# The low part of a split weight chunk, made by an adding DMA instead of by GpSimd

## The chip, the cores and the metric

The kernel runs on one core of a Trainium2 chip. The metric is device time in microseconds (us) from one launch to its end; lower is better. The kernel before takes 1719.38 us (median of three runs, 1719.3 to 1720.42).

## The reference, cut to what matters

One layer of a decoder block on 512 tokens of width 1024: a token-mixing half (gated mixer, sliding-window attention, output projection, layer norm), then a PEER layer that picks 16 of 128 x 128 = 16384 one-neuron experts for each of 8 heads. The change lies in the PEER layer:

```python
q = (xb @ w_pq).reshape(-1, PEER_HEADS, PEER_QDIM)
s1 = jnp.einsum('thd,hkd->thk', q1, sub_k1)          # and s2
v1, i1 = lax.top_k(s1, PEER_TOPK)                    # and v2, i2
cand = v1[..., :, None] + v2[..., None, :]
sc, ci = lax.top_k(cand, PEER_TOPK)
g = jax.nn.softmax(sc, axis=-1)
act = jax.nn.gelu(jnp.einsum('thkd,td->thk', peer_u[e], xb))
return jnp.einsum('thk,thkd->td', g * act, peer_v[e])
```

## The kernel before, in words

Three of the four blocks of 128 tokens (384 tokens) are computed densely: all 16384 experts are applied to them, and the gates g of the experts that were not picked are zero. The table `peer_u` is cut into 128 chunks of 128 experts ("U chunks"), and `peer_v` likewise ("V chunks"). The fourth block of tokens gathers its rows of both tables by indirect DMAs from GpSimd (`ru`, `rv`) late in the program.

Every product is made of three matmuls in a format that keeps fewer bits than f32. A weight chunk is loaded as f32 (`raw`, 128 x 1024, 512 KB), ScalarE (ACT) copies it to the short format (`hi`), and the low part `lo = raw - hi` is made by an elementwise subtraction. `load_split2` does this; the flag `last["pool"]` says whether GpSimd (POOL, line 456) or VectorE (DVE, line 458) subtracts. The tiles rotate over 4 buffers of `raw`, 3 of `hi` and 3 of `lo`. TensorE (PE) then runs 8 times `hi*h2Thi` (L62), `hi*h2Tlo` (L63), `lo*h2Thi` (L64), and ACT applies gelu; while the top-k runs, `U_chunk` also stores the activations to memory (`Ad`, 192 KB, a DMA that ACT issues). SP issues the loads of `raw`, each as soon as the buffer of four chunks earlier has been read for the last time.

The order on each engine is fixed when the program is built. The part in question runs in these steps:

- 16 query projections (`query`, `scores`), with GpSimd subtracting.
- The top-k of all heads, some 250 small steps on DVE (`topk`, lines 533 to 582). Beside it PE computes U chunks: chunks 0 and 1 were made earlier, chunk 2 is issued with the last of the queries, and chunks 3 to 32 follow. GpSimd subtracts for all 31.
- `softmax` (lines 589 to 595: a subtraction on DVE, an exp on ACT, three DVE steps), and `end_topk`, after which DVE subtracts again.
- `spread` (lines 615 to 656): PE transposes the picked indices and gates (`ptg`), ACT copies them (`iT`, `gT`), DVE builds one-hot tiles (`oh`), PE multiplies them (`psg`), ACT copies the result out (`stg`). U chunks 33 and on run beside it, 21 of them with their activations kept in SBUF (`U_resident`).
- The remaining U chunks with the V chunks, and beside them the gathers.

Of the kernel before, what the change touches and what calls it, by code (L numbers as in the profile page):

```python
# [8 lines left out]
F32 = mybir.dt.float32  # L9
# [4 lines left out]
AF = mybir.ActivationFunctionType  # L14
ALU = mybir.AluOpType
# [39 lines left out]
def block_kernel(ctx, tc, I, out):  # L55
    nc = tc.nc
    PS = bass.MemoryType.PSUM

    def mm3(ps, pairs):
        n = len(pairs)  # L60
        for i, (l, r) in enumerate(pairs):
            nc.tensor.matmul(ps, l.hi, r.hi, start=(i == 0), stop=False)  # L62
            nc.tensor.matmul(ps, l.hi, r.lo, start=False, stop=False)  # L63
            last = nc.tensor.matmul(ps, l.lo, r.hi, start=False, stop=(i == n - 1))  # L64
        return last
# [43 lines left out]
    with ExitStack() as fr:  # L109
# [288 lines left out]
        for hh in range(2):  # L398
            for t in range(NT):
# [13 lines left out]
                for kh in range(2):  # L413
# [5 lines left out]
                    for k4 in range(4):  # L419
                        k = 4 * kh + k4  # L420
                        if k < NEV:
                            nc.scalar.activation(hf[:, k4, :], pt[:, k4 * P:(k4 + 1) * P], AF.Identity,
                                                 scale=G2c[:, k:k + 1], bias=B2c[:, k:k + 1])
# [11 lines left out]
    last = {}  # L435

    def behind(ins, other):

        tc.add_manual_dep(ins.ins, other.ins.name,
                          mybir.DependencyInfo(mybir.DependencyClass.NoSync, mybir.DependencyReason.DATA))  # L440
# [4 lines left out]
    def load_split2(src, nm, pool=None):  # L445
        raw = pw.tile([P, NK * P], F32, name=f"raw{nm}", tag="raw", bufs=4)
        last["dma"] = nc.sync.dma_start(raw, src)
        hi = (pool or pw).tile([P, NK * P], F32R, name=f"hi{nm}", tag="hi", bufs=1 if pool else 3)
        lo = (pool or pw).tile([P, NK * P], F32R, name=f"lo{nm}", tag="lo", bufs=1 if pool else 3)
        h = nc.scalar.activation(hi, raw, AF.Copy)  # L450
        if "expn" in last:
            last["expn"] -= 1
            if last["expn"] == 0:
                behind(last["exp"], h)
        if last.get("pool"):
            last["pool_lo"] = nc.gpsimd.tensor_sub(lo, raw, hi.bitcast(F32))  # L456
        else:
            last["dve"] = nc.vector.tensor_sub(lo, raw, hi.bitcast(F32))  # L458
        return Split(hi, lo)
# [11 lines left out]
    def pump(us):  # L471
        credit[0] += us
        while credit[0] > 0 and bg:
            try:
                credit[0] -= next(bg[0])
            except StopIteration:
                bg.pop(0)
# [38 lines left out]
    def query(h, half):  # L516
        nm = f"{h}_{half}"
        w = load_split2(I["w_pq"][2 * h + half], f"pq{nm}")
        ps = pu.tile([P, S], F32, name=f"psq{nm}", tag="mm", bufs=2)
        wv = Split(w.hi.rearrange("p (k c) -> p k c", k=NK), w.lo.rearrange("p (k c) -> p k c", k=NK))  # L520
        mm3(ps, [(wv[:, k, :], h2T[:, k, :]) for k in range(NK)])
        qt = tp.tile([P, S], F32, name=f"qt{nm}", tag="qt", bufs=2)
        nc.scalar.copy(qt, ps)
        return qt

    def scores(h, half, qt):
        pss = pq.tile([P, NT, P], F32, name=f"pssc{h}_{half}", tag="s", bufs=2)
        for t in range(NT):
            nc.tensor.matmul(pss[:, t, :], qt[:, t * P:(t + 1) * P], subk[:, half, h, :], start=True, stop=True)
        nc.scalar.copy(sall[:, 2 * h + half, :, :], pss)  # L530
# [67 lines left out]
    def topk_head(h):  # L598
        return topk(f"h{h}_", DENSE, lambda half, j: sall[:, 2 * h + half, j, :],
                    lambda a: a[:, 0:DENSE, 16 * h:16 * h + 16])  # L600
# [92 lines left out]
    def U_resident(i):  # L693

        w = load_split2(I["uT"][i], f"U{i}")
        ps = pu.tile([P, SD], F32, name=f"psU{i}", tag="mm", bufs=2)
        wv = Split(w.hi.rearrange("p (k c) -> p k c", k=NK), w.lo.rearrange("p (k c) -> p k c", k=NK))
        last["U"] = mm3(ps, [(wv[:, k, :], h2T[:, k, 0:SD]) for k in range(NK)])
        slot, n = res["tile"][:, len(res["ids"]), :], res["spread"]
        if n < SD:  # L700
            nc.scalar.activation(slot[:, n:], ps[:, n:], AF.Gelu)
        if n:
            a = actp.tile([P, SD], F32, name=f"act{i}", tag="act", bufs=4)
            nc.scalar.activation(a[:, 0:n], ps[:, 0:n], AF.Gelu)
            nc.vector.tensor_mul(slot[:, 0:n], slot[:, 0:n], a[:, 0:n])
        res["ids"].append(i)

    def U_chunk(i, keep_act):
        w = load_split2(I["uT"][i], f"U{i}")
        ps = pu.tile([P, SD], F32, name=f"psU{i}", tag="mm", bufs=2)  # L710
        wv = Split(w.hi.rearrange("p (k c) -> p k c", k=NK), w.lo.rearrange("p (k c) -> p k c", k=NK))
        last["U"] = mm3(ps, [(wv[:, k, :], h2T[:, k, 0:SD]) for k in range(NK)])
        a = actp.tile([P, SD], F32, name=f"act{i}", tag="act", bufs=4)
        nc.scalar.activation(a, ps, AF.Gelu)
        if not keep_act:
            nc.scalar.dma_start(Ad[i], a)
        return a
# [86 lines left out]
    bg.append(rows_h2())  # L804
    qt = query(0, 0)
    for j in range(16):
        nxt = query((j + 1) // 2, (j + 1) % 2) if j < 15 else U_chunk(NPRE, False)
        scores(j // 2, j % 2, qt)
        qt = nxt
        if j % 2 == 1:  # L810
            bg.append(topk_head(j // 2))
        pump(QPUMP)
# [5 lines left out]
    def end_topk():  # L818
        tk.close()
        last["pool"] = PLO > 1  # L820
        res["stack"] = ExitStack()
        rp = res["stack"].enter_context(tc.tile_pool(name="rp", bufs=1, side="right", reuse_waits="tile"))
        res["tile"] = rp.tile([P, NRES, SD], F32, name="res")
        res["ids"] = []
        res["first"] = cur[0] + 1
        res["spread"] = 0
        return
        yield

    def end_spread():  # L830
# [3 lines left out]
        yield  # L834

    bg += [topk_last(), softmax(), end_topk(), spread(), end_spread()]
    gt = gather()
    n_g = 0
# [140 lines left out]
```

## Time and profile before

| what | value |
|---|---|
| median of three runs | 1719.38 us |
| the profiled execution | 1727.59 us, span 1725.9 us |
| PE busy | 1668.0 us, 97% of the span |
| DVE busy | 1353.8 us, 78% |
| ACT busy | 685.9 us, 40% |
| POOL busy | 481.5 us, 28% |
| granted TensorE clock | 0.991 of full speed, mean |

The profile is of one execution, which took 8.2 us longer than the median of the runs without a profile; its durations are compared with each other, and a difference is then carried over to the median. Shares over the whole span are averages of stages with different limits. Matmuls are pipelined, so a matmul's duration is not the time that it costs: that is the distance from one start to the next. Times in the rows are microseconds from the start of the span.

### The profile page before, as it was taken

How to read it: one execution, taken by the hardware profiler on the slowest of the kernel's cores; microseconds unless marked ns; L12 is line 12 of the kernel's file. 1: busy time of each engine (PE TensorE's matmuls, PEld its weight loads, DVE VectorE, ACT ScalarE, POOL GpSimd, SP SyncE). 2: the span in 40 equal slices, each digit the busy share in tenths (PEclk: the TensorE clock that was granted, in tenths of full speed). 3: DMA queues.
4: the chain of work that ended last, by engine and by line, in shares of the span. 5: the costliest groups of instructions: out<-in, count | busy, mean ns of one | idle time of the engine just before them, and what ended most of it. 6: DMA issues, size and time to landing. Idle time of an engine off the chain costs nothing.

```text
span 1725.9 us, 23559 instructions
## 1 busy us (share of the span) xinstructions
PE 1668.0 (97%) x8658; PEld 1442.8 (84%) x8658; DVE 1353.8 (78%) x2509; ACT 685.9 (40%) x1095; POOL 481.5 (28%) x334
## 2 busy tenths in 40 slices
PE   6999999999999999899999999999999999989997
PEld 3765777788788999899998789999999999978886
DVE  6467786454589999999978888778787888878787
ACT  3467632233343333355543233333333333333333
POOL 2000000000043455400014444444454545531202
PEclk9999999999999999999999999999999999999999
DMA  7602257642252355556699999999899999899982
GB/s 269 201 1 74 98 196 245 219 146 86 77 189 78 103 173 172 191 206 224 211 321 365 363 325 340 320 338 351 312 337 324 326 345 324 311 351 316 305 282 86
DMA packets 162071, 409.92 MB, mean 238 GB/s; under 512 B 22337, under 2 KB 69473, under 8 KB 161698
## 3 DMA queue, kind: packets, MB, share of 16 engines
q1 hardware_dynamic: 112178, 245.35, 42.3%
q0 software_dynamic: 36960, 134.50, 21.6%
q10 hardware_dynamic: 12816, 28.55, 4.3%
q8 instruction: 68, 1.11, 0.3%
q14 instruction: 49, 0.40, 0.1%
HBM read 377.07 MB, written 31.01 MB: 236 GB/s over the span
## 4 chain that ended last, share of the span: by engine, by line
PE 55%; DVE 18%; DMA 5%; issue 4%; POOL 2%; ACT 0%; SPq 0%; DVEq 0%; POOLq 0%; ACTq 0%
PE acc L801 8%; PE acc L800 8%; PE acc L797 8%; PE psU L64 7%; PE psU L62 6%; PE psU L63 6%; DMA wa<-in_w_ada_dram 2%; POOL ru L667 2%; DMA ru<-in_peer_u_dram,idx 1%; DMA rawV<-in_peer_v_dram 1%; PE pso L63 1%; PE pso L64 1%; PE psga L64 1%; PE psga L62 1%; PE pspa L64 1%
## 5 line engine op out<-in xcount | busy, mean ns | idle before, releaser
L64 PE MATMUL psU<-h2Thi,loU 128*128 128x384 f32 x1008 | 340.6, 338 | 5.4 <-DVE loU L458 5.3
L62 PE MATMUL psU<-h2Thi,hiU 128*128 128x384 f32 x1008 | 340.8, 338 | 0.0
L63 PE MATMUL psU<-h2Tlo,hiU 128*128 128x384 f32 x1008 | 339.3, 337 | 0.0
L797 PE MATMUL acc<-hiV,wh 128*128 128x512 f32 x768 | 300.1, 391 | 4.5 <-ACT wh L782 4.5
L800 PE MATMUL acc<-loV,wh 128*128 128x512 f32 x768 | 301.5, 393 | 1.5 <-DVE loV L458 1.5
L801 PE MATMUL acc<-hiV,wl 128*128 128x512 f32 x768 | 301.1, 392 | 0.3 <-DVE wl L783 0.3
L667 POOL DMA_INDIRECT ru<-in_peer_u_dram,idx x128 | 159.0, 1242 | 360.6 <-DVE ru L671 341.2
L680 POOL DMA_INDIRECT rv<-in_peer_v_dram,idx x128 | 176.4, 1378 | 247.9 <-DVE facc L686 226.6
L458 DVE TENSOR_TENSOR loV<-rawV,hiV 128x1024 fp32r<-128x1024 f32 x128 | 156.4, 1222 | 101.2 <-ACT hiV L450 100.9
L450 ACT ACTIVATE hiV<-rawV 128x1024 fp32r<-128x1024 f32 x128 | 135.1, 1055 | 224.2 <-PE psU L63 184.1
L450 ACT ACTIVATE hiU<-rawU 128x1024 fp32r<-128x1024 f32 x126 | 134.0, 1063 | 194.5 <-PE psU L63 105.5
L64 PEld LDWEIGHTS psU<-h2Thi,loU 128*128 128x128 f32 x1008 | 190.4, 189 | 7.7 <-DVE loU L458 7.6
L63 PEld LDWEIGHTS psU<-h2Tlo,hiU 128*128 128x128 f32 x1008 | 190.6, 189 | 2.6
L62 PEld LDWEIGHTS psU<-h2Thi,hiU 128*128 128x128 f32 x1008 | 190.4, 189 | 2.6
L797 PEld LDWEIGHTS acc<-hiV,wh 128*128 128x128 f32 x768 | 144.9, 189 | 33.7 <-ACT wh L782 5.1
L671 DVE SCALAR_TENSOR_TENSOR ru<-ru,h2n 128x1024 f32<-128x1024 f32 x128 | 154.4, 1221 | 22.0 <-DMA ru<-in_peer_u_dram,idx 21.8
L800 PEld LDWEIGHTS acc<-loV,wh 128*128 128x128 f32 x768 | 144.8, 189 | 32.0 <-DVE loV L458 3.1
L801 PEld LDWEIGHTS acc<-hiV,wl 128*128 128x128 f32 x768 | 144.8, 189 | 31.1 <-DVE wl L783 0.7
L686 DVE SCALAR_TENSOR_TENSOR facc<-rv,wg,facc 128x1024 f32<-128x1024 f32 x126 | 159.4, 1278 | 11.7 <-DMA rv<-in_peer_v_dram,idx 11.7
L456 POOL TENSOR_TENSOR lopq<-rawpq,hipq 128x1024 fp32r<-128x1024 f32 x16 | 40.7, 2544 | 325.1 <-ACT hipq L450 325.1
L782 ACT ACTIVATE wh<-wf 128x384 fp32r<-128x384 f32 x107 | 56.2, 526 | 183.4 <-DVE wf L778 100.5
L458 DVE TENSOR_TENSOR loU<-rawU,hiU 128x1024 fp32r<-128x1024 f32 x95 | 115.7, 1218 | 1.4 <-ACT hiU L450 1.4
(628 smaller groups left out, 2942.4 us busy)
## 6 DMA issues: line engine op xcount, KB each, us to landing
rawU<-in_uT_dram SPq DMA_DIRECT2D x128, 512.0 KB
rawV<-in_peer_v_dram SPq DMA_DIRECT2D x128, 512.0 KB
wa<-in_w_ada_dram SPq DMA_DIRECT2D x48, 512.0 KB
G<-Gd SPq DMA_DIRECT2D x11, 1536.0 KB
Gd<-stg ACTq DMA_DIRECT2D x24, 592.0 KB
rawpq<-in_w_pq_dram SPq DMA_DIRECT2D x16, 512.0 KB
Ad<-act ACTq DMA_DIRECT2D x38, 192.0 KB
ar<-Ad SPq DMA_DIRECT2D x9, 768.0 KB
```

The costliest lines, as they stand in the source:

```text
L62: nc.tensor.matmul(ps, l.hi, r.hi, start=(i == 0), stop=False)
L63: nc.tensor.matmul(ps, l.hi, r.lo, start=False, stop=False)
L64: last = nc.tensor.matmul(ps, l.lo, r.hi, start=False, stop=(i == n - 1))
L450: h = nc.scalar.activation(hi, raw, AF.Copy)
L458: last["dve"] = nc.vector.tensor_sub(lo, raw, hi.bitcast(F32))
L667: d = nc.gpsimd.indirect_dma_start(out=rows, out_offset=None, in_=I["peer_u"], in_offset=bass.IndirectOffsetOnAxis(ap=idx[:, s:s + 1], axi ...
L671: paced(nc.vector.scalar_tensor_tensor(rows, rows, 1.0, h2n, op0=ALU.mult, op1=ALU.mult, accum_out=wg[:, s:s + 1]))
L680: nc.gpsimd.indirect_dma_start(out=rows, out_offset=None, in_=I["peer_v"], in_offset=bass.IndirectOffsetOnAxis(ap=idx[:, s:s + 1], axis=0))
L686: paced(nc.vector.scalar_tensor_tensor(fa, rows, wg[:, s:s + 1], fa, op0=ALU.mult, op1=ALU.add))
L797: m = nc.tensor.matmul(acc, l.hi, r.hi, start=st, stop=False)
L800: nc.tensor.matmul(acc, l.hi, r.lo, start=False, stop=False)
L801: nc.tensor.matmul(acc, l.lo, r.hi, start=False, stop=sp_)
```

## The change

While the top-k runs (from chunk 2 to chunk 32), `load_split2` makes `lo` in another way. ACT writes `-hi` into `lo` (a scaled copy, from `hi`), and a DMA issued by GpSimd adds `raw` to it, from SBUF to SBUF. GpSimd's subtraction is not made for these 31 chunks. The 16 query chunks keep it. All other instructions stay.

```diff
+        if last.get("dma_lo"):
+            nc.scalar.activation(lo, hi.bitcast(F32), AF.Copy, scale=-1.0)
+            last["pool_lo"] = nc.gpsimd.dma_start(lo.bitcast(F32), raw, accum_op=ALU.add)
-        if last.get("pool"):
+        elif last.get("pool"):
             last["pool_lo"] = nc.gpsimd.tensor_sub(lo, raw, hi.bitcast(F32))
...
     for j in range(16):
+        last["dma_lo"] = j == 15
...
     def end_topk():
+        last["dma_lo"] = False
```

The orders of PE, DVE and SP are the same in both kernels. On ACT, in the middle of the top-k, one chunk before is a copy to `hi` of a chunk, the gelu of the chunk three earlier (`act`), and the issue of the store of that one (`Ad`):

```order
L450 ACTIVATE hiU13_5131<-rawU13_5129 128x1024
L714 ACTIVATE act10_5012<-psU10_4987 128x384
L716 DMA Ad_77<-act10_5012 128x384
L450 ACTIVATE hiU14_5178<-rawU14_5176 128x1024
L714 ACTIVATE act11_5064<-psU11_5039 128x384
```

Now the negative copy stands between the gelu and the store:

```order
L450 ACTIVATE hiU13_5142<-rawU13_5140 128x1024
L717 ACTIVATE act10_5021<-psU10_4996 128x384
L456 ACTIVATE loU13_5143<-hiU13_5142 128x1024
L719 DMA Ad_77<-act10_5021 128x384
L450 ACTIVATE hiU14_5190<-rawU14_5188 128x1024
L717 ACTIVATE act11_5074<-psU11_5049 128x384
```

So ACT has one instruction more in each of the 31 chunks, and the low part of chunk 13 is begun behind the gelu of chunk 10. On POOL, the same chunks before:

```order
L456 TENSOR_TENSOR loU13_5132<-rawU13_5129,hiU13_5131 128x1024
L456 TENSOR_TENSOR loU14_5179<-rawU14_5176,hiU14_5178 128x1024
L456 TENSOR_TENSOR loU15_5227<-rawU15_5224,hiU15_5226 128x1024
```

and now:

```order
L457 DMA loU13_5143<-rawU13_5140 128x1024
L457 DMA loU14_5191<-rawU14_5188 128x1024
L457 DMA loU15_5240<-rawU15_5237 128x1024
```

Each subtraction has become the issue of one DMA in the same place.

## Rows read from the trace of the kernel before

**Rows 1.** Busy time by engine, granted clock, DMA share and rate in stretches.

```profile
588.20:718.20 130.00, 130.00 (x755) 130.00 (x755) 129.62 (x541) 46.83 (x66) 71.65 (x29) 1.00 0.48 163
718.20:728.60 10.40, 6.03 (x23) 5.38 (x22) 10.19 (x16) 3.48 (x5) 5.87 (x4) 0.67 0.60 206
...
760.00:790.00 30.00, 28.62 (x247) 27.26 (x246) 30.00 (x40) 16.14 (x33) 0.00 (x0) 1.00 0.63 222
```

**Rows 2.** DVE, groups by line and shape, 588 to 716 us: busy, mean ns.

```profile
L578 DVE TENSOR_TENSOR ohlh__4887<-ohlh__4887,ixfh__4885 128x768 f16<-128x768 f16 x1 | 3.2, 3164 | 0.0
...
L581 DVE TENSOR_TENSOR ohlh__4630<-ohlh__4630 128x384 f16<-128x384 f16 x1 | 2.6, 2560 | 0.0
...
L552 DVE TENSOR_TENSOR candh__4822<-v1h__4681,v0h__4680 128x48 f32<-128x48 f32 x1 | 1.9, 1950 | 0.0
...
L581 DVE TENSOR_TENSOR ohlh__4425<-ohlh__4425 128x384 f16<-128x384 f16 x1 | 0.3, 346 | 0.0
...
L552 DVE TENSOR_TENSOR candh__4559<-v1h__4481,v0h__4480 128x48 f32<-128x48 f32 x1 | 0.2, 183 | 0.0
```

**Rows 3.** Timeline, one U chunk on ACT, POOL: start us, us, instruction [idle before <-releaser].

```profile
689.20 1.06 ACT L450 ACTIVATE hiU<-rawU 128x1024 fp32r<-128x1024 f32 x1 [2.72 <-PE psU L63]
...
690.17 0.47 ACT L714 ACTIVATE act<-psU 128x384 f32<-128x384 f32 x1
...
690.34 2.41 POOL L456 TENSOR_TENSOR loU<-rawU,hiU 128x1024 fp32r<-128x1024 f32 x1 [1.75 <-ACT hiU L450]
...
690.67 0.33 ACTq L716 DMA_DIRECT2D Ad<-act  x1
...
693.36 1.06 ACT L450 ACTIVATE hiU<-rawU 128x1024 fp32r<-128x1024 f32 x1 [2.72 <-PE psU L63]
```

**Rows 4.** Timeline, end of the top-k, PE, ACT and DVE.

```profile
716.91 0.63 ACT L590 ACTIVATE gs<-gs 128x512 f32<-128x512 f32 x1
...
721.04 0.45 PE L64 MATMUL psU<-h2Thi,loU 128*128 128x384 f32 x1 [2.05 <-DVE loU L458]
...
722.03 0.68 DVE L593 TENSOR_REDUCE z<-gs 128x32 f32<-128x512 f32 x1
...
723.14 0.69 DVE L595 TENSOR_TENSOR gs<-gs,z 128x512 f32<-128x512 f32 x1
...
723.98 0.45 PE L615 MATMUL ptg<-ident,gs 128*128 128x128 f32 x1 [2.32 <-DVE gs L595]
...
724.46 0.37 ACT L617 CAST iT<-ptg 128x256 f16<-128x256 f32 x1 [3.28 <-PE ptg L615]
...
724.54 0.52 PE L64 MATMUL psU<-h2Thi,loU 128*128 128x384 f32 x1
...
724.86 0.52 PE L62 MATMUL psU<-h2Thi,hiU 128*128 128x384 f32 x1
```

**Rows 5.** DMA issues of GpSimd: duration ns min/median/max, first and last start.

```profile
L206 POOL DMA_DIRECT2D kd<-kd x1: 755/755/755, 58.9 to 58.9; - x1
...
L667 POOL DMA_INDIRECT ru<-in_peer_u_dram,idx x128: 933/1012/1967, 720.1 to 1228.5; - x128
```

**Rows 6.** Stretches around two kinds of DMA; the last two columns: share, GB/s.

```profile
59.20:60.20 1.00, 1.00 (x6) 0.83 (x5) 0.00 (x0) 0.97 (x3) 1.00 (x2) 1.00 0.00 0
60.20:61.20 1.00, 1.00 (x6) 0.81 (x5) 0.00 (x0) 1.00 (x3) 0.05 (x1) 1.00 0.77 168
61.20:62.20 1.00, 0.91 (x6) 0.57 (x5) 0.39 (x1) 1.00 (x3) 0.00 (x0) 1.00 0.43 94
648.90:649.90 1.00, 1.00 (x8) 1.00 (x7) 1.00 (x2) 0.14 (x1) 1.00 (x1) 1.00 0.83 333
592.60:705.80 113.20, 113.20 (x658) 113.20 (x657) 113.10 (x504) 39.28 (x55) 66.34 (x27) 1.00 0.51 172
```

**Rows 7.** Waits of SP's DMA queue, 560 to 710 us: total, times, longest.

```profile
SPq L447 <- POOL loU L456: 125.0, 31, 6.0
```

## The prediction

> **What bounds the kernel now.** I read the stretches first, to find which engine waits beside the top-k and just after it. While chunks 2 to 32 are computed (588 to 718 us), PE is busy for all 130 us and DVE for 129.6 [rows 1]: two engines that do not wait for each other, since PE multiplies U chunks and DVE sorts. Then come 10.4 us in which PE is busy for 6.0 only and the clock granted to it is 0.67 of full, a mean of its two levels of 2.4 and 1.2 GHz, and after that both are near full again [rows 1]. So the time of the top-k is set by PE, and what DVE is late with is paid in those 10.4 us.
>
> Second, DVE by line and shape, since an engine that is full need not be working. Fourteen of its steps between 588 and 716 us take 1.95 to 3.16 us, while other instances of the same line and shape take 0.18 to 0.95. The pair at L581 shows it best: 2560 ns against 346 for the same 128x384 [rows 2]. Each surplus is 1.7 to 2.2 us, a little below one GpSimd subtraction (2.41 us [rows 3]), as it would be if the step had to wait for that subtraction to end. The fourteen together come to 29.6 us.
>
> Third, the timeline of the 10.4 us. PE waits 2.05 us for the low part of chunk 33, which DVE can make only when its top-k is over, and 2.32 us for the gates `gs` after softmax [rows 4]. Behind these gaps its matmuls start 0.32 us apart [rows 4]; in the top-k a chunk of 24 takes 4.16 us, so 0.173 each [rows 3].
>
> **The change part by part.**
>
> *The subtractions go (31 times 2.41 us of POOL).* POOL's time itself is worth nothing: it waits for ACT before each subtraction [rows 3]. What is worth something is DVE. Without a GpSimd instruction that reads two tiles, I take the fourteen steps back to their short forms: DVE ends its top-k some 29 us earlier, near 690 us and not 719. That is well ahead of PE, so even a PE that is 20 us late would find it done. The low part of chunk 33 is then ready, and so is everything in softmax before the exp. The exp does not move: ACT has it behind the gelu of chunk 31, and it ends at 717.54 [rows 4]. The three DVE steps after it took 1.80 us (722.03 to 723.83 [rows 4]), so the gates are there at 719.35. PE wants them four matmuls into chunk 33, at about 718.95. Of the two stalls 0.4 us is left.
>
> The gain: in the stretch of 10.4 us PE starts 23 instructions [rows 1]; 3 are transposes of some 0.13 us and 20 are matmuls, 3.9 us of work at full clock. 6.5 us are lost there, gaps and slow matmuls together; less 0.4, the gain is 6.1 us. Does the spread that follows pass it on? ACT's copy `iT` waited 3.28 us for the gates [rows 4] and starts earlier too, with DVE's first one-hot tiles behind it. From 760 to 790 us DVE is busy for 30.0 of 30 us and PE for 28.6 [rows 1], but DVE's stream there begins with products that PE makes, so it moves with PE. I take all 6.1, with 3.3 as the lower end (the spread moves only as far as `iT` does).
>
> *31 negative copies on ACT.* By the copy to `hi`, 1.06 us each. In its period of 4.16 us ACT is idle for 2.72 before the next `hi` [rows 3]; the new copy fits with 1.6 to spare. Its store of the activations starts 1.06 us later, and nobody near waits for it. Cost 0; were that idle time gone, it would be up to 1.06 a chunk.
>
> *31 adding DMAs.* Two questions: is a low part in time, and can the DMA engines carry it?
>
> In time: count from the start of a `hi` copy, 689.20 in the rows. The gelu ends 1.44 later, the negative copy at 2.5. GpSimd issues the DMA in about 1.0 (the median of its gathers of the same 512 KB, 1012 ns; the plain 128 KB copy `kd` took 755 [rows 5]). The `kd` copies are issued from 58.9 us on, and nothing moves until 60.2 [rows 6], so the first bytes come 1.3 after the start of the issue: 3.8. The `hi` copies start when PE has finished a chunk's L63, and its low part is wanted two whole periods later plus the three matmuls before the next L64: 8.8. That leaves 5.0 us for the transfer. The load of `raw` for the chunk four later now waits for the DMA, not for POOL [rows 7]: about 3 us later than now, with over three periods (12.5 us) until ACT wants it. Nothing else stands behind it in SP's queue at that time.
>
> The engines: the trace has no adding DMA, so its price is bounded. From below by moving 512 KB once at the rate of a `raw` load: 333 GB/s at a share of 0.83 [rows 6] is 401 GB/s while busy, 1.31 us. From above by the `kd` copies, the only ones from SBUF to SBUF: 256 KB took shares of 0.77 and 0.43 us [rows 6], 1.2 us, so 512 KB take 2.4, and if it counts twice because an add reads two tiles, 4.8. I take the reading of both tiles at the rate of the loads, 2.62 us: `kd` uses only 64 partitions on either side, the loads all 128, and so does the add. With the load (512 KB) and the store (192 KB), 1.80 us at the same 401 GB/s, one period then carries 1.77 MB in 4.42 us, against PE's 4.16. 0.25 us too much, over the 29 chunks from 4 to 32 (2 and 3 lie beside the queries), is 7.3 us. The transfer of 2.62 has 2.4 us of slack before PE notices (5.0 less 2.6), so PE ends the top-k about 4.9 us late. The bounds for this term: 0 with 3.1 us at the lower end, and (1.80 + 4.8 - 4.16) x 29 - 0 = 71 us at the upper. Below nothing it can't be.
>
> On the price the Trainium skill, *Collectives: The Full Stack* (section "The bandwidth ceiling: the fold count and why AG ≠ RS ≠ AR"), says that a reducing DMA runs at half the rate of a copy because it reads two sources; by that the add would also take 2.62 us, and no run here shows it. *DMA: Bandwidth & Descriptors* ("Where 436 GB/s comes from") puts the fabric's ceiling at 435 GB/s; by that figure, as an estimate, a period carries its 1.77 MB in 4.07 us, PE is never late, and the sum would be -6.1.
>
> *Sum.* -6.1 + 4.9 = -1.2 us on the profiled execution: a span of 1725.9 becomes 1724.7, its 1727.6 in all become 1726.4. Nothing in the difference hangs on the profiling, so the median of 1719.4 becomes 1718.2.
>
> **The rivals.**
>
> *The DMA engines carry it.* The busy share holds waiting within transfers, which a second queue may fill. For it: the share is only 0.51 now [rows 6]. Against: 0.51 x 4.16 = 2.1 us, and 2.6 more is over a period. Then PE is not late: 1719.4 - 6.1 = 1713.3.
>
> *The adding DMA is slow, and the DMA queue takes PE's place.* One mechanism: the engines add at about half the rate that I took. Price at `kd`'s rate counted twice: 71 - 6.1 = +65, 1784 us, and more if adding is slower still. It decides from a transfer in which (1.80 + x - 4.16) x 29 - 2.4 exceeds 6.1 + 3.4, so x = 2.8 us, hardly above my value. For it: `kd`, the nearest in kind, is the slowest per byte. Against: its 64 partitions.
>
> *The gain isn't there.* If the long DVE steps wait for something else than the subtraction, or GpSimd's issue holds DVE up as long, PE's stalls stay and only the lateness counts: about 1719.4 to 1724. Against it: the surplus of each step is so near to one subtraction.
>
> **How the numbers follow.** What a measurement can tell from no change is about 0.2%, 3.4 us. My forecast, with the engines about full: 0.45, its own range 1713 to 1728 (never late; or 2.1 + 2.62 without any overlap, 14 us late); of it 0.12 is faster, 0.23 same, 0.10 slower. The engines carry it: 0.25, nearly all faster. The slow add: 0.23, all slower. No gain: 0.07, of which 0.02 same. Together faster 0.36, same 0.26, slower 0.38. The range runs from 1711 to 1757: below lies little (the whole 6.1 and some of the later waits), above the part of the slow add with more than about 4 us a transfer.
>
> **What would show it.** DVE: the fourteen steps at their short times, and the top-k over near 690. PE: no wait for the low part of chunk 33 and the clock not falling there. ACT: its `hi` copies still released by PE, 4.16 us apart or a little more; the distance is the DMA's answer. The share of the DMA engines in the top-k near 1.0; at 0.8 with chunks 4.16 us apart the first rival is right, with chunks 5 us and more apart the second. Long DVE steps beside POOL's issues would show the third. A gain or loss that arises outside 588 to 860 us would make my account wrong.

## The result, and the profile after

The changed kernel takes 1737.05 us (median of four runs, 1734.4 to 1742.32), the kernel before 1719.9 beside it (four runs, 1719.3 to 1723.05): ratio 1.010, 95% interval 1.0072 to 1.0127. A second comparison with more runs (seven against twenty, below) gave 1.0067 [1.0042, 1.0093]. So the change costs 11 to 17 us. Forecast were 1718.2 us and a gain of 1.2. The gain came as forecast; the loss beside the top-k was three times as large as I took it, and a second loss at the very end was not foreseen.

The stretches of the changed kernel (length, busy time of PE, of PE's weight loads (PEld), DVE, ACT, POOL, then granted clock, DMA share, GB/s), cut at the same times as [rows 1]:

```profile
588.20:718.20 130.00, 120.72 (x673) 117.02 (x672) 94.17 (x507) 66.97 (x85) 23.77 (x28) 0.99 1.02 259
718.20:728.60 10.40, 9.84 (x57) 9.43 (x56) 2.45 (x2) 4.75 (x7) 4.98 (x5) 1.00 1.03 314
...
760.00:790.00 30.00, 28.61 (x268) 27.32 (x268) 30.00 (x40) 17.60 (x37) 0.00 (x0) 1.00 0.65 235
```

Three things stand against [rows 1]. The DMA engines' share in the top-k has gone from .48 to 1.02 (the view adds up the times of all packets over 16 engines, so it can pass 1). DVE is busy for 94 us of 130, not 129.6, and the step that stands right behind its top-k comes early:

```profile
L667 DVE SCALAR_TENSOR_TENSOR idx<-i1s,i2s x1: 291/291/291, 682.6 to 682.6; 128x128 int32<-128x128 f32 x1
```

(one line of the kernel: duration min/median/max, first and last start; the same step started at 719.6 before). Executions differ by some us in when they reach the top-k, so I count from PE's first matmul of chunk 3 (593.35 us before, 589.94 now): DVE is through after 92.6 us, where it took 126.2. The pair of [rows 2] at 2560 and 346 ns has become short throughout, as in this head, where one of the three took 2557 before:

```profile
L584 DVE TENSOR_TENSOR ohlh__4473<-ohlh__4473 x3: 207/259/355, 594.2 to 594.9; 128x384 f16<-128x384 f16 x1, 128x192 f16<-128x192 f16 x1, 128x96 f16<-128x96 f16 x1
```

PE, which never waited in that stretch, lacks 9.3 us there. The waits of 580 to 740 us name what it lacked (total us, times, longest):

```profile
ACT hiU L450 <- PE psU L63: 74.6, 33, 5.5
...
PEld psU L64 <- DMA loU<-rawU: 13.9, 13, 2.2
PE psU L64 <- DMA loU<-rawU: 9.8, 10, 1.9
```

PE now waits for low parts that the adding DMA has not yet brought, and for no DVE step at all. These waits are not the whole loss. Behind the longest of them, at 609 us, the granted clock fell to its lower level of 1.2 GHz for 3.4 us (a row of PE's timeline, then a stretch with the columns above):

```profile
609.28 0.56 PE L64 MATMUL psU<-h2Thi,loU 128*128 128x384 f32 x1 [1.89 <-DMA loU<-rawU]
...
609.20:612.80 3.60, 3.52 (x11) 3.52 (x12) 3.60 (x21) 0.08 (x1) 0.87 (x1) 0.53 1.06 256
```

Some eleven matmuls start 0.32 us apart there and not 0.173, an estimated 1.6 us. ACT's `hi` copies, the answer to [rows 3], still wait for PE, all but one, often 4.16 us apart:

```profile
643.07 1.06 ACT L450 ACTIVATE hiU<-rawU 128x1024 fp32r<-128x1024 f32 x1 [1.77 <-PE psU L63]
644.04 0.47 ACT L717 ACTIVATE act<-psU 128x384 f32<-128x384 f32 x1
644.41 1.05 ACT L456 ACTIVATE loU<-hiU 128x1024 fp32r<-128x1024 f32 x1
...
647.23 1.06 ACT L450 ACTIVATE hiU<-rawU 128x1024 fp32r<-128x1024 f32 x1 [1.77 <-PE psU L63]
```

The tile of low parts tells how long an add takes from its issue until it has landed:

```profile
L457 POOL DMA_DIRECT2D loU<-rawU x31: 862/872/957, 574.9 to 718.9; - x31
...
DMA to landing us min/median/max: 4.7/6.8/9.1
```

I had 3.9 (1.3 until bytes move and 2.62 of transfer). SP's loads wait for it now, as forecast, and the answer to [rows 7], here for 560 to 720 us, is

```profile
SPq L447 <- DMA loU<-rawU: 141.7, 30, 11.3
```

which costs nothing by itself: PE and ACT wait for no load of `raw`. The queues show where the price was wrong. From 610 to 700 us, in the kernel before (packets, MB, share of 16 engines' time; q1 carries the loads of `raw`, q10 the stores of activations):

```profile
q1 hardware_dynamic: 3168, 11.54, 38.9%
q10 hardware_dynamic: 3056, 4.18, 12.8%
```

and in the changed kernel, where q0 is the adding DMA:

```profile
q0 software_dynamic: 2687, 9.76, 56.7%
q1 hardware_dynamic: 2734, 9.96, 33.4%
q10 hardware_dynamic: 2725, 3.73, 11.4%
```

To get the engines' time per chunk, multiply a share by the period. Before: .389 x 4.16 = 1.62 us for a load and .128 x 4.16 = 0.53 for a store, 2.15 together. After, with a period of 4.67 us (140.05 us from chunk 3 to 33, 30 chunks): 2.65 us for an add, 1.56 and 0.53 beside it, 4.74 us in all. The add is about what I took (2.62). Load and store are 2.15, not the 1.80 that I got from one microsecond of a load at full rate.

Last, the closing instructions of the program. In the kernel before (the DRAIN instructions of GpSimd's sequencer at the last line, min/median/max ns):

```profile
L975 POOLq DRAIN  x3: 40/102/6403, 1718.1 to 1725.6; - x3
```

and in the changed one:

```profile
L980 POOLq DRAIN  x3: 46/102/10034, 1723.4 to 1733.9; - x3
```

The longest of the three starts behind GpSimd's last work and everything else waits for it before the program ends. 6.4 us of it lay beside the last stores of the result; 10.0 us do not, and the program ends 6.3 us after DVE's last step, where it was 3.3.

### The profile page after: what moved, and what is told of

It reads as the page before. It is cut to its first block, busy times and chain, and to the rows that moved or that the text cites. A ratio compares the mean times of both kernels' runs of the same rounds, so it can differ in the third digit from the quotient of the medians.

```text
span 1734.2 us, 23659 instructions
## 1 busy us (share of the span) xinstructions
PE 1669.9 (96%) x8658; PEld 1442.0 (83%) x8658; DVE 1318.8 (76%) x2509; ACT 715.7 (41%) x1126; POOL 432.9 (25%) x334
## 4 chain that ended last, share of the span: by engine, by line
PE 46%; issue 14%; DMA 6%; DVE 3%; POOL 2%; ACT 0%; SPq 0%; DVEq 0%; POOLq 0%; ACTq 0%
PE acc L803 7%; PE acc L804 7%; PE acc L800 7%; PE psU L64 7%; PE psU L62 6%; PE psU L63 6%; DMA loU<-rawU 2%; DMA ar<-Ad 2%; POOL ru L670 2%; PE psq L62 2%; PE psq L64 2%; PE psq L63 2%; DMA ru<-in_peer_u_dram,idx 1%; DMA rawV<-in_peer_v_dram 1%; DVE loV L461 1%
```

## The experiments

Theory A, the load: the DMA engines have more to do per chunk than PE, and PE's lateness is their surplus times the chunks. Theory B, found in the first traces: the closing drain on GpSimd grows with the DMAs that it has issued. Rivals: the lateness comes from the latency or the issue of an adding DMA whatever its size; and the gain at chunk 33 is not DVE's.

Four places of the traces decide, so here they are for all runs. "3 to 33" is the time from PE's first matmul of chunk 3 to that of chunk 33, "33 to 35" likewise; "end" is how much later than in the kernel before the program ends behind DVE's last step. "Sum" adds the three differences from the kernel before; "measured" is the ratio of the times less 1, times 1722 us, with its interval.

| run | DMA share, 588 to 718 us | 3 to 33 | 33 to 35 | drain | end | sum | measured us |
|---|---|---|---|---|---|---|---|
| before | .48 | 125.04 | 15.48 | 6.40 | | | |
| before again | .47 | 125.03 | 15.38 | 6.40 | 0 | | |
| changed | 1.02 | 140.05 | 8.83 | 10.03 | 3.05 | +11.4 | +17.2 [12.4, 21.9] |
| changed again | 1.02 | 137.70 | 8.54 | 10.03 | 3.05 | +8.8 | +11.5 [7.2, 16.0] |
| every second | .79 | 128.66 | 8.92 | 8.28 | 1.29 | -1.6 | -1.0 [-3.4, 1.5] |
| plain copy | .83 | 126.97 | 8.88 | 8.94 | 1.95 | -2.7 | +0.3 [-2.1, 2.8] |
| no store | 1.01 | 131.18 | 8.88 | 10.03 | 3.05 | +2.6 | +3.6 [0.2, 6.9] |
| every fourth | .67 | 125.03 | 8.93 | 7.34 | 0.35 | -6.2 | -7.6 [-10.3, -5.0] |
| half width | .87 | 133.07 | 8.53 | 10.03 | 3.05 | +4.1 | +5.2 [2.6, 7.7] |
| small copies | .50 | 126.02 | 21.12 | 8.94 | 1.95 | +8.6 | +16.2 [12.2, 20.3] |
| every eighth | .56 | 125.03 | 12.74 | 6.85 | 0 | -2.7 | -2.6 [-4.8, -0.5] |
| every third | .73 | 125.30 | 8.93 | 7.58 | 0.60 | -5.7 | -4.7 [-7.1, -2.2] |

### The kernel before, once more

> The kernel before, once more, for a second trace of it. The first trace was of an execution 8.2 us above the median, and reached chunk 2 at 588.3 us where the changed kernel, whose instructions are the same up to there, reached it at 584.9. If that is a matter of the execution, this trace reaches chunk 2 near 585 us and the total is near 1720. If the first trace is typical, it reaches it at 588. In both cases the U chunks beside the top-k are 4.16 us apart and chunk 33 waits for VectorE again.

No edit. Chunk 2 is reached at 587.8 us and the chunks beside the top-k are 4.16 us apart, as in the first trace. 1726.12 us under the profile; 29 runs of the same kernel on that chip gave a median of 1721.95 (1718.07 to 1728.13). Chunk 33's stall and the drain are as in the first trace, so these two places repeat to 0.1 us and the whole does not: two profiles of one kernel reach the last 40 V chunks 1.1 to 3.9 us apart, and in stages that the change does not touch. The stretch from 1520 to 1560 us had a granted clock of 0.91 in one and 1.00 in the other. Differences of a few us are therefore read from the stage, not from the span.

### The adding DMA for every second chunk

> The adding DMA for the even chunks of 2 to 32 only, GpSimd subtracts for the odd ones. Theory (the DMA engines are full: load and store take 2.12 us of them in a period, the add 2.66): two periods carry 2 x 2.12 + 2.66 = 6.9 us of 8.3, so the chunks stay 4.16 us apart, no wait of TensorE for the adding DMA, and VectorE, with half its waits for GpSimd gone, ends its top-k some 15 us earlier, still before TensorE: the gain of 6.5 us behind the top-k comes in full, 1719.9 - 6.5 = 1713.4. Rival (the chain of copy, issue and transfer is too long for three buffers, whatever the load): the even chunks are still 1 to 2 us late, 15 of them, the net 8 to 24 us worse than 1713.

```diff
-        if last.get("dma_lo"):
+        if last.get("dma_lo") and int(nm[1:]) % 2 == 0:
```

1720.24 us, ratio 0.9994 [0.998, 1.0009]: neither gain nor loss, where I expected 1713.4. All of the gain at chunk 33 is there (8.92 against 15.48) with half of the adds. But PE still loses 3.6 us before it, at a mean share of .79, to waits like these:

```profile
PEld psU L64 <- DMA loU<-rawU: 3.8, 4, 2.2
PE psU L64 <- DMA loU<-rawU: 2.5, 3, 1.9
```

A mean share below 1 is not enough for nothing to be late. Another 1.3 us go into the drain.

### A plain copy in place of the add

> The DMA copies raw into lo in place of adding it: the low parts of chunks 2 to 32 are then the whole chunk. Same issue by GpSimd, same bytes written, half the bytes read. Theory (full DMA engines, and the add costs twice a copy): 2.12 + 1.33 = 3.45 us of 4.16, so the DMA share falls from 1.02 to about 0.83, the chunks are 4.16 us apart, and only the gain of 6.5 us is left: 1713.4. Rival 1 (the long chain): the landing stays late and the chunks are 4.5 us apart and more, 1725 or above. Rival 2 (the add itself is slow per packet, not by its bytes): as the theory in time, but the share falls by much more than half of the add's part.

```diff
-            last["pool_lo"] = nc.gpsimd.dma_start(lo.bitcast(F32), raw, accum_op=ALU.add)
+            last["pool_lo"] = nc.gpsimd.dma_start(lo.bitcast(F32), raw)
```

It leaves the add out: `lo` becomes `raw`. 1723.33 us, ratio 1.0002 [0.9988, 1.0016]: the share is .83 as expected, the time is not the 1713.4 that I expected. From 610 to 700 us its software queue shows:

```profile
q0 software_dynamic: 3134, 11.43, 32.6%
```

.326 of 90 us on 16 engines for 3134 packets is 150 ns a packet; the adding ones of the changed kernel take 304 (.567, 2687). The add costs twice the copy. The Trainium skill, *Collectives: The Full Stack* ("The bandwidth ceiling: the fold count and why AG ≠ RS ≠ AR"), gives the reduce step of a ring collective half of a copy's rate because it reads two sources; the page speaks of collectives alone, and for this add inside one core the trace agrees. With the copy PE is late by 1.9 us and not 15.0, with as many DMAs in the same queue: the doubled transfer makes the loss, not their number. The copy's issue is shorter too (0.54 us against 0.87), so this run alone does not rule out the issue; the next one changes no issue of GpSimd. Of the 2.7 us that the stages then leave as a gain, the runs show none; their interval ends at -2.1, and I have no place in the trace for the rest.

### No stores of the activations

> As the changed kernel, without the stores of the activations of chunks 4 to 32 (192 KB each); later those chunks read the stored rows of chunks 0 to 3. Theory (full DMA engines): the store took some 0.53 us of a period, so 4.78 - 0.53 = 4.25 us of DMA against 4.16 of TensorE: the chunks come 4.16 to 4.3 us apart, TensorE ends the top-k 0 to 4 us late, and the total is 1713 to 1718. Rival (the long chain, not the load of the engines): chunks still 4.68 us apart and 1737.

```diff
-        if not keep_act:
+        if not keep_act and not 4 <= i <= 32:
             nc.scalar.dma_start(Ad[i], a)
```

The 29 stores of chunks 4 to 32 are left out, and the later loads of them read another part of `Ad`. 1724.66 us, ratio 1.0021 [1.0001, 1.004]. PE's lateness falls from 15.0 to 6.1 us, where I expected 0 to 4: a store of 0.53 us (the queue's share above) in 29 chunks is 15.4 us of load, and 8.9 come back. The two queues that are left still fill the engines:

```profile
q0 software_dynamic: 2972, 10.86, 69.7%
q1 hardware_dynamic: 2889, 10.50, 31.9%
```

With 4.37 us a chunk that is 3.05 for an add and 1.39 for a load: when it meets only loads, the add's packets stay longer in the engines (338 ns a packet). So the price of a transfer in a share is itself a matter of what else runs. For theory A's cause this run speaks plainly, though its size was missed: it changes no adding DMA and no instruction of GpSimd, and takes away more than half of the lateness.

### The changed kernel, once more

> The changed kernel once more, with more runs. Load theory (the DMA engines have 4.68 us of work per chunk of 4.16): PE is 15 us late between chunks 4 and 33 again, 6.6 us come back at chunk 33. Drain theory, new from the first traces: the program's closing drain on GpSimd takes 10.0 us and not 6.4, of which 3.0 us show at the end. Together +15.0 - 6.6 + 3.0 = +11.4 us, ratio 1.0066. If the first comparison's +17 us holds instead (1.010), something that these stages don't show is still missing.

No edit. 1734.35 us against 1723.24, ratio 1.0067 [1.0042, 1.0093], +11.1 us by the medians: the expectation from load and drain was 1.0066. PE is 12.7 us late, not 15.0, and the drain is again 10.03. In this trace the clock does not fall in the top-k, which is an estimated 1.6 of the 2.3 us between the two. Its own stages add up to 8.8 us, so it is partly luck that the total meets the expectation. The first comparison's 17 us lie above its stages' sum of 11.4; its four runs of the kernel before (1719.3 to 1723.05) lie in the lower half of what the same kernel took in the twenty runs here (1718.78 to 1730.67).

### The adding DMA for every fourth chunk

> Adding DMA only for chunks 4, 8, ... 32 (8 of 31), GpSimd subtracts the others. Load theory: DMA share in the top-k near .48 + .16 = .64, PE late by some 1.7 us (8 times the 0.21 us a chunk of the run with every second chunk). The top-k's steps on VectorE end some 7.6 us earlier (8/31 of 29.5), enough for all of the 6.6 us at chunk 33. Drain theory: closing drain 6.40 + 8 x 0.117 = 7.3 us, 0.9 us at the end. Sum -6.6 + 1.7 + 0.9 = -4.0 us, ratio 0.9977. Rival (the gain at chunk 33 goes by the share of chunks changed): 6.6 x 8/31 = 1.7 us of gain, sum +0.9, ratio 1.0005.

```diff
-        if last.get("dma_lo"):
+        if last.get("dma_lo") and int(nm[1:]) % 4 == 0:
```

1716.83 us against 1723.24, ratio 0.9956 [0.994, 0.9971]. This beats both kernels. PE is not late at all (125.03 us, as before), where I expected 1.7; all of the gain at chunk 33 is there, and the drain costs 0.35. Its stretches:

```profile
588.20:718.20 130.00, 129.83 (x753) 129.49 (x752) 125.36 (x536) 54.35 (x73) 63.06 (x33) 1.00 0.67 207
718.20:728.60 10.40, 10.40 (x84) 10.24 (x82) 9.56 (x10) 5.44 (x12) 0.00 (x0) 1.00 0.59 235
```

The second row is the place where the kernel before had PE at 6.03 us and a clock of 0.67 [rows 1]. Here PE is full at full clock. DVE is still nearly full beside it: eight subtractions fewer on GpSimd took about 7 us off its surplus (each step's time above the short one of its line and shape, by my count 32 us before and 25 here). Counted from PE's start of chunk 3 it is through with its top-k after 117.4 us, where it took 126.2, and that suffices. An add that meets no other add lands in

```profile
DMA to landing us min/median/max: 4.5/4.6/5.1
```

against 6.8 in the changed kernel. This speaks against the first rival: eight adds with their issue and their 4.6 us each make PE late by nothing.

### Half the width

> All 31 chunks keep an adding DMA, but of half the columns (512 of 1024); GpSimd subtracts the other half. Load theory: 2.1 us of load and store plus half of 2.66 us a chunk, 3.45 of 4.16 us, share .83; PE less than 1 us late between chunks 4 and 33; VectorE's surplus about half (16 us), which still gives the 6.6 us at chunk 33. Rival (each adding DMA costs by its issue and its latency, whatever its size): 15 us late as with the whole width, ratio 1.007. Drain theory by the number of DMAs or of their rows: closing drain 10.0 us, +3.0 at the end, sum -3.0, ratio 0.998; by bytes: 8.2 us, +1.2 at the end, sum -4.8, ratio 0.997.

```diff
+            w = NK * P // 2
-            nc.scalar.activation(lo, hi.bitcast(F32), AF.Copy, scale=-1.0)
-            last["pool_lo"] = nc.gpsimd.dma_start(lo.bitcast(F32), raw, accum_op=ALU.add)
+            nc.scalar.activation(lo[:, :w], hi[:, :w].bitcast(F32), AF.Copy, scale=-1.0)
+            nc.gpsimd.dma_start(lo[:, :w].bitcast(F32), raw[:, :w], accum_op=ALU.add)
+            last["pool_lo"] = nc.gpsimd.tensor_sub(lo[:, w:], raw[:, w:], hi[:, w:].bitcast(F32))
```

1727.97 us, ratio 1.003 [1.0015, 1.0045]: slower, where I expected 0.997 to 0.998. PE is 8.0 us late, not under 1. More than half of that is one place. GpSimd's timeline at the end of the top-k:

```profile
708.72 1.28 POOL L459 TENSOR_TENSOR loU<-rawU,hiU 128x512 fp32r<-128x512 f32 x1 [2.04 <-ACT hiU L450]
711.06 1.06 POOL L672 DMA_INDIRECT ru<-in_peer_u_dram,idx  x1 [1.05 <-issue]
712.10 1.00 POOL L458 DMA_DIRECT2D loU<-rawU  x1
```

and PE's first matmul behind it:

```profile
718.97 0.44 PE L64 MATMUL psU<-h2Thi,loU 128*128 128x384 f32 x1 [2.61 <-DMA loU<-rawU]
```

The last add stands behind the first gather, so it is issued at 712.1 although its operands were ready at 709.5 and GpSimd was free at 710.0. Chunk 32 takes 8.8 us on PE instead of 4.3: 4.5 us, of which an estimated 1.6 are matmuls at the lower clock, granted from 720.2 to 723.6 us behind this wait. The other 3.5 lie at the chunks before, at a share of .87. The share alone does not give the lateness: at .79 it was 3.6 us with every second chunk, at .83 1.9 with the plain copy. The drain is 10.03 us as with whole adds: it goes by the number of DMAs and not by their bytes.

### Small copies beside the subtractions

> The subtraction stays on GpSimd as in the kernel before; behind each of the 31 subtractions GpSimd issues one DMA that copies one column (4 bytes of each of 128 partitions) to a tile that nothing reads. No load to speak of, VectorE not freed, so the top-k and chunk 33 as before. Drain theory by the number of DMAs or rows: the closing drain takes 8.9 to 10.0 us, the time is 1.9 to 3.0 us longer, ratio 1.001 to 1.002. By bytes or by the tile they write: drain 6.4 us, ratio 1.000.

```diff
+            last["pool_lo"] = nc.gpsimd.tensor_sub(lo, raw, hi.bitcast(F32))
+            c = last["junk"] = last.get("junk", -1) + 1
+            nc.gpsimd.dma_start(junk[:, c:c + 1], raw[:, :1])
```

(in place of the negative copy and the add). 1739.74 us, ratio 1.0094 [1.0071, 1.0118], far more than the 2 to 3 us that I expected. The drain is

```profile
L982 POOLq DRAIN  x3: 40/102/8935, 1727.1 to 1736.6; - x3
```

exactly that of the plain copies of 512 KB each (8.94): again by number. The surprise is chunk 33. Counted from PE's start of chunk 3, DVE is through with its top-k after 132.8 us, 6.6 later than before, and the stall grows by 5.7:

```profile
726.09 0.69 PE L64 MATMUL psU<-h2Thi,loU 128*128 128x384 f32 x1 [7.62 <-DVE loU L462]
729.03 0.45 PE L620 MATMUL ptg<-ident,gs 128*128 128x128 f32 x1 [1.93 <-DVE gs L600]
```

These are the two waits of [rows 4], the first now 7.62 us and not 2.05. So DMA issues that bring DVE nothing make its top-k later, and PE pays for most of those us. Whether the issues themselves hold DVE up, or only move the subtractions against its steps, this run does not tell. Nor do the three places account for all of it: 7.6 us of the 16.2 are left. Of these 4.5 lie between V chunks 24 and 80, which take 469.7 us here and 465.1 to 465.2 in every other run, at full clock and without a wait of PE: the matmuls of `wh` and `wl` start 231 to 237 ns apart and not 227 to 230. This kernel alone holds one tile more (`junk`); whether that moved other tiles and slowed these matmuls, no run shows. The rest stays open.

### The adding DMA for every eighth and for every third chunk

> Adding DMA only for chunks 8, 16, 24 and 32. VectorE's surplus in the top-k falls by 0.87 us per changed chunk (31.9 to 25.2 us with eight), so here by 3.5 us. One-to-one theory (each us by which the top-k on VectorE ends earlier is one us less of PE's wait at chunk 33, up to 6.6): gain 3.3 us at chunk 33, closing drain 6.40 + 4 x 0.117 = 6.87 us (+0.5), PE not late before chunk 33. Sum -2.8 us, ratio 0.9984; from chunk 33's start to chunk 35's 12.1 us, where the kernel before has 15.4 and the run with every fourth chunk 8.9. Rival (the wait goes as a whole or not at all, since it is a low clock or another engine that sets it): 15.4 or 8.9 us there.

> Adding DMA for chunks 3, 6, ... 30 (10 of 31). VectorE some 8.7 us earlier, of which chunk 33 can take 6.6. DMA share .48 + 10/31 x .64 = .69. Load theory: PE not late, as with every fourth chunk (.67): sum -6.6 + 1.2 (drain 7.57 us) = -5.4 us, ratio 0.997. Rival (each adding DMA costs PE 0.21 us from the first on): 2.1 us late, sum -3.3 us, ratio 0.998.

The edits are that of every fourth chunk, with 8 and with 3. Every eighth: 1720.96 us against 1723.61, ratio 0.9985 [0.9972, 0.9997], expected 0.9984. From chunk 33 to 35 it takes 12.74 us (expected 12.1), between the 15.4 of no add and the 8.9 of eight; the rival that the stall goes wholly or not at all falls. DVE is through with its top-k 2.2 us earlier than before, where I expected 3.5, and the stall is 2.7 us shorter. PE's wait for the gates is still there:

```profile
720.05 0.30 PE L618 MATMUL ptg<-ident,gs 128*128 128x128 f32 x1 [2.31 <-DVE gs L598]
```

Every third: 1719.08 us, ratio 0.9973 [0.9959, 0.9987], expected 0.997. PE is 0.3 us late (the rival had 2.1), and the two adds more than with every fourth chunk buy nothing. Between the two the runs do not decide; their intervals overlap.

## Why the prediction was wrong

**DVE's surplus: right.** The fourteen long steps are gone. Counted from the start of chunk 3 the top-k on DVE was over 33.6 us earlier (92.6 us against 126.2), where I had 29.

**The gain at chunk 33: right.** Forecast 6.1 us, measured 6.6 and 6.9. Its cause is shown from several sides: four adds give 2.7 us, eight, ten or sixteen all of it, and a DVE that is made later by 6.6 us loses 5.7. The stages behind it pass the gain on, as I took it: from chunk 35 to DVE's last step it is 989.1 and 988.2 us in the two traces of the changed kernel, 988.7 and 987.9 in those of the kernel before.

**ACT's negative copies at no cost: right as far as the runs show.** Its `hi` copies are still released by PE, 1.77 us after ACT fell idle. No run isolates them; the plain copy keeps all 31, and there PE is late by 1.9 us in all.

**The step that failed: "With the load (512 KB) and the store (192 KB), 1.80 us at the same 401 GB/s".** I took the rate of one microsecond of a load for both. Their time on the engines is 2.15 us a chunk: 1.62 for the load, where my rate gives 1.31, and 0.53 for the store, where it gives 0.49. So it is the load that I mispriced: over 90 us it does not keep the rate of its best microsecond. I had this number twice, as the share .51 of [rows 6] times 4.16 in the first rival and in the upper end of my own range, and put the smaller one into the sum. With 2.15 and my own 2.62 a period is 4.77 us, (4.77 - 4.16) x 29 less the slack of 2.4 is 15.3 us late, and 15.0 and 12.7 were measured. That it meets the first of them so closely is luck: by the 19 adds that are issued from 610 to 700 us an add took 2.7 us (.567 of 90 us, by 19), which gives 17 in the same sum; an add takes 4.6 us to land even alone and not 3.9, so the slack was smaller; and 1.6 us of the 15.0 are the lower clock, which I had nowhere in this stage. The size holds, the tenths do not. The term came out as 4.9 because it is a small difference of two large ones: 0.35 us in 4.4 tripled it. The run without stores shows that the load of the engines makes the lateness, and the plain copy that most of it comes with the second half of the add's price.

The estimate from *DMA: Bandwidth & Descriptors* of the Trainium skill ("Where 436 GB/s comes from"), 4.07 us a period at 435 GB/s and PE never late, falls with it: the period was 4.59 to 4.67.

**Not in the sum: the drain.** 3.0 us at the end that no row of before pointed to, since there the drain lay beside the last stores. I had written that a loss outside 588 to 860 us would make my account wrong; by that test too it was incomplete.

**The rivals.** "The DMA engines carry it" is out: the share is 1.02. "The adding DMA is slow" has the right place and sign and the wrong price: the add was not slower than I took. The gain was there. With the right load and the drain the sum is -6.6 + 15.3 + 3.0 = +11.7, beside +11.5 measured in the larger comparison and +17.2 in the first; the stages of the two traces alone add up to 8.8 and 11.4, so what is left of the first comparison, 5.8 us, stays open. The result lies above the 1728 that ended the range of my own case.

## What to carry to other kernels

Price a queue that is to be filled by the share that its present traffic has, not by bytes over the best rate, and read the lateness as a surplus times a count: near a full period a tenth decides between gain and loss. Where a change pays through one stall of limited length, apply it only as often as the stall needs: eight of 31 chunks brought all of the gain here and 0.35 us of the loss. Look at what stands at the very end of the program too, since work moved to another queue may be settled there.

## What the runs showed of the hardware that I had not expected

- The closing drain on GpSimd takes 6.40 us without these DMAs and 0.117 us more for each adding DMA (16: 8.28; 31: 10.03), 0.082 for each plain one (31: 8.94), whatever their size. Four adds gave 6.85, eight 7.34, ten 7.58.
- An adding DMA from SBUF to SBUF takes the engines twice the time of a copy: 304 ns a packet against 150, 2.65 us against 1.38 for 512 KB (.326 of a period of 126.97 / 30 us).
- With 31 small DMA issues on GpSimd beside its subtractions DVE was through with its top-k 6.6 us later, while 31 adding DMAs without subtractions left it at its short times.
- One late low part can cost PE more than its wait: behind waits of 1.9 and 2.6 us (609 us in the changed kernel, 719 us with half the width) the granted clock fell to 1.2 GHz for 3.4 us, an estimated 1.6 us each; waits of 1.7 us in the second trace of the changed kernel and of 1.9 us with every second chunk were not followed by it.
